# Two-layer decoder trunk on one core: attention scores in visits of four heads, PSUM banks split four and four, sums of squares and their columns at other places

## The chip, the cores and the metric

The kernel runs on one core of a Trainium2 chip. Time is the device time of one execution in microseconds (us). The core's engines appear in the profile as PE (matmul; PEld is its loading of stationary operands), DVE (VectorE), ACT (ScalarE), POOL (GpSimd) and SP (SyncE, which here only issues DMAs). Each engine runs its own queue in order; semaphores make one wait for another.

## The reference, cut to what matters

A sequence of 256 tokens with 1024 channels goes through two layers. Each is: half an FFN step, an attention mixer, half an FFN step, every one on an RMS-normalised copy and added to the stream.

```python
def rmsnorm(x, g):
    return x * lax.rsqrt(jnp.mean(x * x, axis=-1, keepdims=True) + RMS_EPS) * g
def swiglu(h, w_gate, w_up, w_down):
    return (jax.nn.silu(h @ w_gate) * (h @ w_up)) @ w_down
h = h + 0.5 * swiglu(rmsnorm(h, g1), ...)      # D_FF 2816
h = h + mixer(rmsnorm(h, g2))                  # 16 heads of 64
h = h + 0.5 * swiglu(rmsnorm(h, g3), ...)
```

Mixer A (layer 0) is a merged mixture of dilated causal windows; with 256 tokens it comes to one softmax with a mask that holds the logarithm of how many patterns allow a pair. Mixer B (layer 1) is causal attention with keys and values that are projected from the stream after layer 0. A final RMS norm ends it. All is float32.

## The kernel before, in words

**Numbers.** Every float32 operand of a product is split into two parts of a faster format: `hi` is a rounded copy that ACT makes (tiles `wh` for weights, first half of `x`, `pT` and so on), `lo` is the rest, which DVE makes by a subtraction (`wl`). A product is hi*hi + hi*lo + lo*hi, three matmuls into one accumulator (`product`, L189) or, in the FFN, one matmul of 512 columns (hi weights against both halves of x) and one of 256 (lo weights against the hi half; `products_t`, L198: L203 and L206).

**FFN.** `ffn_blocks` (L351) goes over 22 blocks of 128 hidden channels, in pairs that share a load. For each block `both` (L357) makes a gate and an up accumulator: eight hi matmuls of gate, eight hi of up, eight lo of gate, eight lo of up. `close` (L363), traced one block later, adds the two halves of each accumulator (`joined`, L332: a copy by ACT at L335, an add by DVE at L336, after which the bank is free), multiplies by the norm's row, and makes the product silu(gate)*up. The first pair (f = 0) is different: its four accumulators are open at once, and the loop over the eight blocks of x is the outer one. Three of the four come from the pool `accp`, one from `trp`. `quartered` (L449) is the down projection; some of its block pairs go by seven products of quarter blocks, so eight accumulators are open there.

**Norms.** `Norm.scale` makes the two parts of gain*x. `Norm.square` (L234) squares a block on ACT (L237, L240) and POOL adds it to the sum `ss` (L241). `Norm.finish` (L243) makes the column: two float32 matmuls with 1/D (`col`, L246), an addition of epsilon on DVE (L248), a power -0.5 on POOL (L250, `c`). `Norm.spread` turns the column into a row for the FFN (L257, L258, L260). In the very first FFN (`opening`, L172, and `first`, L805) weights and x come in small DMAs; `first` squares blocks two places behind those that it scales, and blocks 6 and 7 are squared behind the loop.

**Mixers.** `mixer` (L722) writes its order out by hand. `projections` (L789) yields 0.68 for every product of three matmuls with 512 columns; six segments of two token halves (t) with eight products each. `Agenda` (L266) holds calls that are due at a time of this count: `evacuate` (L767) scales the finished half by the norm's column (ACT, tile `rt`; DVE rotates it, L635 to L638), `turn_in` (L752) transposes queries and keys (`qt`, L761), `scores(p)` (L649) makes the scores of heads 2p and 2p+1 in two banks, as 12 matmuls that use 64 rows of the array each, one head on each half (L656), and DVE adds the mask and takes the minimum of the negated scores (L664), which frees the banks. `soften`, `scale`, `turn` (L679, transposes `pt`), `values` (L691, accumulator `po`) follow. The lists in the two calls of `mixer` give the waits, counted from the last `turn_in` of a group of four heads. `out_t` (L591) is the output projection, with four accumulators. `Pieces` (L292) loads and splits the projection's weights; `get` keeps four pieces ahead (`LEAD`).

**PSUM.** Eight banks: five in `accp` (accumulators, `acc`), three in `trp` (turns, scores, columns, rows, `trt`). A tile gets a bank of its pool when one is free.

**Order.** The program is traced in the order of the text. The framework then fills each engine's queue ahead of time: among the instructions that it takes to be ready it picks the one that was traced first. `queued(name)` (L145) binds what is traced under it to be queued behind marked instructions of the same engine; nothing waits for them to end. `marks` (L143) holds the marked ones.

The profile drops the numbers in names: `f_g` and `f_u` are the gate and up accumulators of all four FFNs, f10, f20, f11 and f21; `x_n` the scaled x of any norm.

Of the kernel before, what the change touches and what calls it, by code (L numbers as in the profile page):

```python
# [17 lines left out]
NT = S // P  # L18
# [48 lines left out]
def trunk(ctx: ExitStack, tc: tile.TileContext, a: dict, out: bass.AP):  # L67
# [10 lines left out]
    accp = ctx.enter_context(tc.tile_pool(name="accp", bufs=5, space=PS))  # L78
    trp = ctx.enter_context(tc.tile_pool(name="trp", bufs=3, space=PS))
# [92 lines left out]
    def opening(wg, wu, before):  # L172


        for k, n in OPENING:
# [5 lines left out]
            nc.scalar.activation(wh, raw, AF.Copy)  # L181
# [16 lines left out]
    def products_t(acs, wss, xs, first, last):  # L198


        for ac, ws in zip(acs, wss):
            for i, ((wh, wl), x) in enumerate(zip(ws, xs)):
                nc.tensor.matmul(ac, wh, flat(x), start=first and i == 0, stop=False)  # L203
        for ac, ws in zip(acs, wss):
# [14 lines left out]
    class Norm:  # L219
# [23 lines left out]
        def finish(self):  # L243
# [4 lines left out]
            nc.vector.tensor_scalar_add(v, ps[:, :NT], EPS)  # L248
# [43 lines left out]
    class Pieces:  # L292
# [3 lines left out]
        def __init__(self, specs):  # L296
            self.specs, self.raws, self.parts, self.rest = specs, [], [], []
# [9 lines left out]
        def split(self, i):  # L307

            end = 2 * len(self.specs)
            while len(self.parts) <= min(i, end - 1):  # L310
# [10 lines left out]
                while len(self.rest) > (m < end - 1):  # L321
                    self.rest.pop(0)()
# [28 lines left out]
    def ffn_blocks(name, wg, wu, norm, first=None, beside=(), sums=None, queue=()):  # L351
# [5 lines left out]
        def both(f, pair):  # L357
            acs = [acc(f"{name}_{n}{f}") for n in "gu"]
            cols = slice(f % 2 * P, (f % 2 + 1) * P)
            products_t(acs, [[(wh[:, cols], wl[:, cols]) for wh, wl in w] for w in pair], norm.x, True, True)  # L360
# [33 lines left out]
        for f in range(0, KF, 2):  # L394
# [5 lines left out]
            if f == 0:  # L400
# [8 lines left out]
                if first is not None:  # L409
                    for k in range(KD - 2, KD):  # L410
                        norm.square(k)
                if norm.col is None:
                    norm.finish()
# [35 lines left out]
    def quartered(name, w, acts, sums, weight, collected, tail=2):  # L449
# [6 lines left out]
        c11, c12, m1, m5, m7 = [acc(f"dn_{name}_{n}") for n in ("11", "12", "m1", "m5", "m7")]  # L456
        c21, m6, c22 = [trt(f"dn_{name}_{n}") for n in ("21", "m6", "22")]
# [182 lines left out]
    def attention(agenda, operands, mask, name, blocks):  # L640
# [50 lines left out]
        def values(p):  # L691
            g, b = divmod(p, HG // 2)
            po = acc(f"po_{name}{p}")
# [28 lines left out]
    def mixer(name, segs, plan, wo, mask, after, queue={}):  # L722
# [17 lines left out]
        agenda = Agenda()  # L740
        for norm in {id(norm): norm for norm, _, _ in segs}.values():
            for i in range(len(norm.late)):
                agenda.after(1.5 + 0.5 * i, lambda norm=norm: norm.late.pop(0)())
            if norm.col is None:
                agenda.after(8.1, norm.finish)
# [21 lines left out]
        def evacuate(i, t, r, ac, parts):  # L767
# [17 lines left out]
            for g in sorted(set(turned)):  # L785
                if ("q", g, t) in heads and ("k", g, t) in heads:
                    agenda.after(4.4 - 1.2 * t if i == 0 else 3.2, turn_in, g, t)

        def projections():  # L789
            for i, (norm, x, parts) in enumerate(segs):  # L790
                acs = [acc(f"{''.join(part[0] for part in parts)}_{name}{i}_{t}") for t in range(NT)]
                for k0 in range(0, KD, 4):
                    for t in range(NT):
# [4 lines left out]
                        if k0 + 4 == KD:  # L798
                            evacuate(i, t, norm.col[t], acs[t], parts)
# [5 lines left out]
    def first(k, n):  # L805
# [4 lines left out]
        for i in range(k - 2, k - 2 + n):  # L810
            if i >= 0:
                n0.square(i)
# [14 lines left out]
    def ending(at):  # L827
# [3 lines left out]
          [steps(0, 3.0, 8.0, 11.0, 13.8, 16.5, 19.3), steps(1, 3.0, 8.0, 11.0, 13.8, 16.5, 19.3), steps(2, 4.0, 9.2),  # L831
# [92 lines left out]
```

## Time and profile before

| | |
|---|---|
| runs | 980.27, 980.28, 980.37 us (median 980.28) |
| the profiled execution | 980.13 us, of which the span from first to last instruction is 978.4 |
| PE busy | 967.5 us of the span |
| granted PE clock | 0.998 of full speed |

The stages lie on the span like this (from PE's timeline): opening and f10's gate and up products from 5 us; f10's down projection until 190; mixer a until 308; f20 until 489; f11 until 672; mixer b until 789; f21 and the final norm until 978. A timeline row gives start, duration, engine, line, operation, output<-inputs, shapes, and in brackets how long the engine was idle before it and what ended that. Matmuls overlap: their real pace is read from start to start.

### The profile page before, as it was taken

What the parts mean: (1) busy time and instruction counts of PE and PEld (TensorE: products, weight loads), DVE (VectorE), ACT (ScalarE), POOL (GpSimd) and SP (SyncE); (2) the same over time, 40 slices, a digit from 0 to 9 for tenths busy, and PEclk for the clock granted to TensorE, in tenths of its full rate; (3) what the DMA queues carried; (4) which work ended last, traced back from release to release, by engine and by line L of the source; (5) the groups of instructions that cost most, each with busy time, mean ns of one, the idle gap of its engine ahead of it and who ended that gap; (6) DMA issues with size and microseconds to landing.
All of it is one profiled execution on the core that took longest, in us unless ns stands there. A gap on an engine that the chain in (4) does not pass through costs nothing.

```text
span 978.4 us, 14860 instructions
## 1 busy us (share of the span) xinstructions
PE 967.5 (99%) x5391; PEld 831.9 (85%) x5391; DVE 813.0 (83%) x1383; ACT 612.7 (63%) x1131; POOL 287.0 (29%) x242
## 2 busy tenths in 40 slices
PE   8999999999999999999999999999999999999997
PEld 6888888878889888888888888888888998888886
DVE  7988899887878788889898888987787878888995
ACT  7655657567777665556576655655677756666561
POOL 3211246132332211146032121612142322112461
PEclk9999999999999999999999999999999999999999
DMA  9875536664334556546755556483734345564341
GB/s 317 259 238 187 197 133 216 219 212 157 133 98 152 180 186 189 184 153 208 256 172 173 172 177 212 169 277 114 249 131 136 116 145 172 186 202 173 130 172 43
DMA packets 126857, 176.00 MB, mean 180 GB/s; under 512 B 3392, under 2 KB 106304, under 8 KB 126784
## 3 DMA queue, kind: packets, MB, share of 16 engines
q1 hardware_dynamic: 125936, 174.01, 53.7%
q10 hardware_dynamic: 848, 1.05, 0.3%
q8 instruction: 42, 0.69, 0.3%
q14 instruction: 31, 0.25, 0.1%
HBM read 173.99 MB, written 1.05 MB: 179 GB/s over the span
## 4 chain that ended last, share of the span: by engine, by line
PE 92%; DVE 4%; ACT 2%; issue 1%; POOL 1%; DMA 0%; SPq 0%; POOLq 0%; DVEq 0%; ACTq 0%
PE f_g L203 16%; PE f_u L203 16%; PE f_u L206 8%; PE f_g L206 8%; PE dn_f_d L196 6%; PE dn_f_d L192 6%; PE dn_f_d L194 6%; PE dn_f_d_m L196 1%; PE dn_f_d_m L194 1%; PE dn_f_d_m L192 1%; PE qk_a L192 1%; PE qk_a L196 1%; PE qk_a L194 1%; DVE x_n L96 1%; PE q_b L192 1%
## 5 line engine op out<-in xcount | busy, mean ns | idle before, releaser
L368 POOL TENSOR_TENSOR j_f_u<-j_f_u,r_n 128x256 f32<-128x256 f32 x88 | 92.3, 1051 | 360.8 <-DVE j_f_u L336 338.0
L203 PE MATMUL f_g<-x_n,wh_f_g 128*128 128x512 f32 x688 | 180.5, 394 | 0.0
L203 PE MATMUL f_u<-x_n,wh_f_u 128*128 128x512 f32 x688 | 177.2, 390 | 0.0
L203 PEld LDWEIGHTS f_u<-x_n,wh_f_u 128*128 128x128 f32 x688 | 129.2, 188 | 27.3
L203 PEld LDWEIGHTS f_g<-x_n,wh_f_g 128*128 128x128 f32 x688 | 124.0, 189 | 22.7
L167 DVE TENSOR_TENSOR wl_f_u<-raw_f_u,wh_f_u 128x1024 fp32r<-128x1024 f32 x86 | 113.1, 1316 | 1.1 <-ACT wh_f_u L166 1.0
L167 DVE TENSOR_TENSOR wl_f_g<-raw_f_g,wh_f_g 128x1024 fp32r<-128x1024 f32 x86 | 104.3, 1230 | 2.8 <-ACT wh_f_g L166 2.8
L206 PE MATMUL f_u<-x_n,wl_f_u 128*128 128x256 f32 x688 | 103.3, 283 | 0.0
L206 PE MATMUL f_g<-x_n,wl_f_g 128*128 128x256 f32 x688 | 102.7, 282 | 0.0
L206 PEld LDWEIGHTS f_g<-x_n,wl_f_g 128*128 128x128 f32 x688 | 96.4, 190 | 6.3
L166 ACT ACTIVATE wh_f_u<-raw_f_u 128x1024 fp32r<-128x1024 f32 x86 | 88.0, 1049 | 12.0 <-PE f_g L203 7.5
L166 ACT ACTIVATE wh_f_g<-raw_f_g 128x1024 fp32r<-128x1024 f32 x86 | 89.6, 1049 | 4.7 <-PE f_g L203 2.8
L206 PEld LDWEIGHTS f_u<-x_n,wl_f_u 128*128 128x128 f32 x688 | 91.6, 192 | 0.0
L366 ACT ACTIVATE j_f_g<-j_f_g 128x256 f32<-128x256 f32 x88 | 36.7, 417 | 87.2 <-DVE j_f_g L365 86.9
L241 POOL TENSOR_TENSOR ss_n<-ss_n,sq_n 128x256 f32<-128x256 f32 x42 | 38.4, 913 | 148.8 <-ACT sq_n L240 146.8
L98 ACT ACTIVATE act_f<-j_f_g 128x256 fp32r<-128x256 f32 x58 | 23.9, 418 | 56.4 <-DVE j_f_g L376 56.4
L376 DVE TENSOR_TENSOR j_f_g<-j_f_g,j_f_u 128x256 f32<-128x256 f32 x58 | 27.9, 487 | 30.1 <-POOL j_f_u L368 30.1
L484 POOL TENSOR_TENSOR sum_f_d_6b<-sum_f_d_6ac,raw_f_d 128x512 f32<-128x512 f32 x4 | 45.5, 11371 | 17.6 <-DVE sum_f_d_6ac L483 13.2
L336 DVE TENSOR_TENSOR j_f_g<-f_g,j_f_g 128x256 f32<-128x256 f32 x88 | 36.6, 416 | 11.9 <-ACT j_f_g L335 11.9
L677 POOL TENSOR_SCALAR sm_b<-sm_b,ls_b 128x128 f32<-128x128 f32 (+1 forms) x32 | 28.5, 907 | 55.7 <-DVE ls_b L675 29.6
L335 ACT ACTIVATE j_f_u<-f_u 128x256 f32<-128x256 f32 x88 | 33.0, 375 | 15.0 <-PE row_n L258 14.0
L365 DVE TENSOR_TENSOR j_f_g<-j_f_g,r_n 128x256 f32<-128x256 f32 x88 | 41.4, 474 | 0.7
(565 smaller groups left out, 2369.3 us busy)
## 6 DMA issues: line engine op xcount, KB each, us to landing
raw_f_d<-in_ffn_w_down_dram SPq DMA_DIRECT2D x44, 1024.0 KB, 4.9
raw_f_g<-in_ffn_w_gate_dram SPq DMA_DIRECT2D x43, 1024.0 KB, 5.2
raw_f_u<-in_ffn_w_up_dram SPq DMA_DIRECT2D x43, 1024.0 KB, 5.2
raw_qka<-in_a_w_qkv_dram SPq DMA_DIRECT2D x16, 512.0 KB, 4.7
raw_va<-in_a_w_qkv_dram SPq DMA_DIRECT2D x4, 1024.0 KB, 5.4
raw_ao<-in_a_w_o_dram SPq DMA_DIRECT2D x4, 1024.0 KB, 4.9
raw_kvb<-in_kv_w_dram SPq DMA_DIRECT2D x8, 512.0 KB, 4.7
raw_qb<-in_b_w_q_dram SPq DMA_DIRECT2D x4, 1024.0 KB, 5.9
```

Source lines behind the costliest of these rows:

```text
L166: nc.scalar.activation(wh, r, AF.Copy)
L167: nc.vector.tensor_sub(wl, r, wh.bitcast(F32))
L192: nc.tensor.matmul(ac, xh, wh, start=first, stop=False)
L194: nc.tensor.matmul(ac, xh, wl, start=False, stop=False)
L196: nc.tensor.matmul(ac, xl, wh, start=False, stop=last)
L203: nc.tensor.matmul(ac, wh, flat(x), start=first and i == 0, stop=False)
L206: nc.tensor.matmul(ac[:, :S], wl, x[:, 0, :], start=False, stop=last and i == len(ws) - 1)
L241: nc.gpsimd.tensor_tensor(self.ss, self.ss, sq, op=ALU.add)
L365: nc.vector.tensor_mul(g, g, norm.row)
L366: nc.scalar.activation(g, g, AF.Silu)
L368: nc.gpsimd.tensor_tensor(u, u, norm.row, op=ALU.mult)
L484: nc.gpsimd.tensor_tensor(b[:, 0], ac[:, 0], raw[:, 3], op=ALU.add)
```

## The change

- **Banks.** `accp` has four buffers for five, `trp` four for three. `po` of `values` moves from `accp` to `trp`; in the down projection the accumulator m7 does.
- **Scores.** The waits of the two `scores` calls of a group become equal for three of the four groups of each mixer (4.5 and 4.5 for 3.0 and 8.0, and so on), so that both calls run one after the other.
- **Columns in the mixers.** The column of the first segment's norm is due at 8.7 for 8.1, that of another norm at 14.0. After it, the DVE splits of `Pieces` are queued behind the column's addition (`behind`). The evacuation is put on the agenda (at once, or 0.6 later where the column isn't traced yet). `turn_in` of the first segment's second half is due 3.6 behind its evacuation for 3.2.
- **Opening.** `first` only scales. All eight squares are traced behind the opening's loop and queued on ACT behind the last weight split there. The column of this norm is traced in block 2, between gate's hi matmuls and up's (`between`).

```diff
-    accp = ctx.enter_context(tc.tile_pool(name="accp", bufs=5, space=PS))
-    trp = ctx.enter_context(tc.tile_pool(name="trp", bufs=3, space=PS))
+    accp = ctx.enter_context(tc.tile_pool(name="accp", bufs=4, space=PS))
+    trp = ctx.enter_context(tc.tile_pool(name="trp", bufs=4, space=PS))
...
@@ opening
-            nc.scalar.activation(wh, raw, AF.Copy)
+            marks["opening"] = [nc.scalar.activation(wh, raw, AF.Copy)]
...
-    def products_t(acs, wss, xs, first, last):
+    def products_t(acs, wss, xs, first, last, between=None):
         for ac, ws in zip(acs, wss):
             for i, ((wh, wl), x) in enumerate(zip(ws, xs)):
                 nc.tensor.matmul(ac, wh, flat(x), start=first and i == 0, stop=False)
+            if between is not None:
+                between()
+                between = None
...
@@ Norm.finish
-            nc.vector.tensor_scalar_add(v, ps[:, :NT], EPS)
+            marks[self.name] = [nc.vector.tensor_scalar_add(v, ps[:, :NT], EPS)]
...
@@ Pieces
-            self.specs, self.raws, self.parts, self.rest = specs, [], [], []
+            self.specs, self.raws, self.parts, self.rest, self.behind = specs, [], [], [], None
...
-                while len(self.rest) > (m < end - 1):
-                    self.rest.pop(0)()
+                with queued(self.behind):
+                    while len(self.rest) > (m < end - 1):
+                        self.rest.pop(0)()
...
@@ ffn_blocks
-            products_t(acs, [[(wh[:, cols], wl[:, cols]) for wh, wl in w] for w in pair], norm.x, True, True)
+            products_t(acs, [[(wh[:, cols], wl[:, cols]) for wh, wl in w] for w in pair], norm.x, True, True,
+                       norm.finish if norm.col is None else None)
...
                 if first is not None:
-                    for k in range(KD - 2, KD):
-                        norm.square(k)
-                if norm.col is None:
+                    with queued("opening"):
+                        for k in range(KD):
+                            norm.square(k)
+                elif norm.col is None:
                     norm.finish()
...
@@ quartered
-        c11, c12, m1, m5, m7 = [acc(f"dn_{name}_{n}") for n in ("11", "12", "m1", "m5", "m7")]
-        c21, m6, c22 = [trt(f"dn_{name}_{n}") for n in ("21", "m6", "22")]
+        c11, c12, m1, m5 = [acc(f"dn_{name}_{n}") for n in ("11", "12", "m1", "m5")]
+        c21, m6, m7, c22 = [trt(f"dn_{name}_{n}") for n in ("21", "m6", "m7", "22")]
...
@@ values
-            po = acc(f"po_{name}{p}")
+            po = trt(f"po_{name}{p}")
...
@@ mixer
+        def column(norm):
+            norm.finish()
+            pieces.behind = norm.name
...
-                agenda.after(8.1, norm.finish)
+                agenda.after(8.7 if norm is segs[0][0] else 14.0, column, norm)
...
-                    agenda.after(4.4 - 1.2 * t if i == 0 else 3.2, turn_in, g, t)
+                    agenda.after(4.4 - 0.8 * t if i == 0 else 3.2, turn_in, g, t)
...
-                            evacuate(i, t, norm.col[t], acs[t], parts)
+                            agenda.after(0.6 if norm.col is None else 0.0,
+                                         lambda t=t, i=i, norm=norm, ac=acs[t], parts=parts:
+                                         evacuate(i, t, norm.col[t], ac, parts))
...
@@ first
-        for i in range(k - 2, k - 2 + n):
-            if i >= 0:
-                n0.square(i)
...
@@ the calls of mixer: a, then b
-          [steps(0, 3.0, 8.0, 11.0, 13.8, 16.5, 19.3), steps(1, 3.0, 8.0, 11.0, 13.8, 16.5, 19.3), steps(2, 4.0, 9.2),
+          [steps(0, 4.5, 4.5, 11.0, 13.8, 16.5, 19.3), steps(1, 4.5, 4.5, 11.0, 13.8, 16.5, 19.3), steps(2, 5.0, 5.0),
            steps(3, 2.4, 5.4) + ending(8.4)],
...
-          [steps(0, 3.0, 8.0, 11.0, 13.8, 17.0, 19.8), steps(1, 4.0, 9.8, 12.4, 15.2, 17.9, 20.7), [],
-           steps(2, 2.2, 4.3) + steps(3, 6.4, 8.5) + ending(10.4)],
+          [steps(0, 4.5, 4.5, 11.0, 13.8, 17.0, 19.8), steps(1, 5.5, 5.5, 12.4, 15.2, 17.9, 20.7), [],
+           steps(2, 2.4, 2.4) + steps(3, 6.4, 8.5) + ending(10.4)],
```

## The prediction

> **What bounds the kernel now.** I read the page first: engine shares, then the chain that ended last.
>
> ```profile
> PE 967.5 (99%) x5391; PEld 831.9 (85%) x5391; DVE 813.0 (83%) x1383; ACT 612.7 (63%) x1131; POOL 287.0 (29%) x242
> PE 92%; DVE 4%; ACT 2%; issue 1%; POOL 1%; DMA 0%; SPq 0%; POOLq 0%; DVEq 0%; ACTq 0%
> ```
>
> The matmul engine is busy almost everywhere, and the chain runs through it for 92%. The change removes no matmul, so all that can be won is PE's idle time and what it loses between matmuls. The second view is the table by stretches (span, then PE's busy time):
>
> ```profile
> 0.00:14.00 14.00, 11.61 (x44) 6.78 (x45) 8.18 (x15) 10.46 (x21) 4.04 (x10) 1.00 0.90 295
> 26.00:132.00 106.00, 106.00 (x613) 93.70 (x612) 92.09 (x159) 66.62 (x124) 21.10 (x20) 1.00 0.65 213
> ```
>
> In the gate and up products PE has no gap in 106 us; in the opening it lacks 2.4 of 14 us. So only the opening, the two mixers and the seams are open. The third view, PE's waits, gives the largest:
>
> ```profile
> PE f_g L206 <- DVE wl L182: 0.8, 1, 0.8
> PE f_g L203 <- ACT wh L181: 0.8, 2, 0.5
> ```
>
> This view leaves out short gaps, so for the mixers I went down to single rows.
>
> **The norms' columns later.** The timeline of PE has, in mixer a and then in mixer b, the last product ahead of the column and the column (start, duration):
>
> ```profile
> 199.44 0.50 PE L196 MATMUL qk_a<-wh_qka,x_n 128*128 128x512 f32 x1
> 200.04 0.61 PE L246 MATMUL col_n<-mean,ss_n 128*128 128x1 f32 x4
> ...
> 681.45 0.39 PE L196 MATMUL kv_b<-wh_kvb,x_kx 128*128 128x512 f32 x1
> 682.41 0.61 PE L246 MATMUL col_n<-mean,ss_n 128*128 128x1 f32 x4 [0.57 <-POOL ss_n L241]
> ```
>
> In the score rows below, matmuls of 512 columns follow each other every 0.23 us. So PE stood 200.04-199.44-0.23 = 0.37 us in a and 682.41-681.45-0.23 = 0.73 us in b, both for the sum of squares on POOL. The new due times put the column one product (three matmuls, 0.68 us) later in a (8.7 for 8.1) and about nine later in b (14.0): the sums are done before, and other products, which have their weights, fill PE. Gain 1.10 us. In a the column is now late for what follows, the queries' first turn:
>
> ```profile
> 205.15 0.39 PE L196 MATMUL v_a<-wh_va,x_n 128*128 128x512 f32 x1
> 205.76 0.63 PE L761 MATMUL qt_a<-ident,rt_a 128*128 128x128 f32 x4 [0.23 <-ACT wh_qka L318]
> ...
> 207.38 0.40 PE L196 MATMUL v_a<-wh_va,x_n 128*128 128x512 f32 x1
> 207.95 0.63 PE L761 MATMUL qt_a<-ident,rt_a 128*128 128x128 f32 x4 [0.18 <-DVE rt_a L638]
> ```
>
> Two waits, 0.38 and 0.34 us, 0.72 together. They end when the rotated heads are there, that is, by column, variance, power, evacuation, rotation. The edit touches this chain twice: the weight splits on DVE are queued behind the variance (new `behind`), so that it no longer waits for a split, and the first turn is due one product later (the evacuation is deferred by 0.6), the second more (0.8 for 1.2). I count both waits as gone. Behind the variance on DVE stand the splits of pieces that are four ahead of their product (LEAD); a hold of one split hides there. Bounds: 0 and 0.72.
>
> **Scores of four heads in one visit.** One visit of today, on PE:
>
> ```profile
> 211.64 0.39 PE L196 MATMUL v_a<-wh_va,x_n 128*128 128x512 f32 x1
> 211.96 0.33 PE L656 MATMUL s_a<-qkh_a 64*128 64x128 f32 x2
> 212.12 0.28 PE L656 MATMUL s_a<-qkl_a,qkh_a 64*128 64x128 f32 x2
> ...
> 212.63 0.28 PE L656 MATMUL s_a<-qkh_a,qkl_a 64*128 64x256 f32 x2
> 212.85 0.50 PE L192 MATMUL v_a<-wh_va,x_n 128*128 128x512 f32 x1
> 213.18 0.39 PE L194 MATMUL v_a<-wl_va,x_n 128*128 128x512 f32 x1
> ```
>
> Going in costs 211.96-211.64-0.23 = 0.09 us; going out 0.11 (the last pair needs about 0.11 of the 0.22 to 212.85) and 0.10 more, since the first product takes 0.33 to the next instead of 0.23. A visit thus carries 0.30 us beside its twelve matmuls. Two visits in one save one such 0.30 and pay a change from pair to pair, which I take as the 0.05 by which the first change inside a visit (0.16) exceeds 0.11. Three of four groups in two mixers: six times 0.25 = 1.50 us. No row has two visits in a row: bounds 0 (no merging) and 6 x 0.30 = 1.80. The eight reductions that follow load DVE in one block instead of two; nothing waits for them soon, since the first turn stays at 11.0.
>
> A fourth turn bank also removes one wait. The last scores of mixer b:
>
> ```profile
> 759.73 0.73 PE L656 MATMUL s_b<-qkh_b 64*128 64x128 f32 x2
> 760.15 0.43 PE L656 MATMUL s_b<-qkl_b,qkh_b 64*128 64x128 f32 x2
> ...
> 759.66 0.42 DVE L664 CUSTOM_DVE_ANT_0 sm_b<-s_b,masks 128x256 f32<-128x256 f32 x1
> ```
>
> The second head starts only when DVE has read the visit before (760.08): 0.42 instead of 0.16 to the next pair, 0.26 us. Mixers together: 1.10 + 0.72 + 1.50 + 0.26 = **3.58 us less**.
>
> **The bank taken from the accumulators.** Each FFN opens with four accumulators at once, three in `accp` and one in `trp`. With five banks, gate and up of block 2 found two free ones. With four, gate 2 takes the last, and up 2 must wait until DVE has read gate 0 (L336). Here stand when up 2 starts, and that read: f11, with PE's next three items (both low halves, the row, block 3), then f20, f21 and the opening.
>
> ```profile
> 503.91 1.98 PE L203 MATMUL f_u<-x_n,wh_f_u 128*128 128x512 f32 x8
> 505.73 1.12 PE L206 MATMUL f_g<-x_n,wl_f_g 128*128 128x256 f32 x8
> 507.64 0.60 PE L258 MATMUL row_n<-diag_n,ones 128*128 128x128 f32 x4
> 508.00 2.09 PE L203 MATMUL f_g<-x_n,wh_f_g 128*128 128x512 f32 x8
> 507.05 0.42 DVE L336 TENSOR_TENSOR j_f_g<-f_g,j_f_g 128x256 f32<-128x256 f32 x1
> ...
> 321.41 1.99 PE L203 MATMUL f_u<-x_n,wh_f_u 128*128 128x512 f32 x8
> 322.18 0.42 DVE L336 TENSOR_TENSOR j_f_g<-f_g,j_f_g 128x256 f32<-128x256 f32 x1
> ...
> 802.96 1.99 PE L203 MATMUL f_u<-x_n,wh_f_u 128*128 128x512 f32 x8
> 803.73 0.42 DVE L336 TENSOR_TENSOR j_f_g<-f_g,j_f_g 128x256 f32<-128x256 f32 x1
> ...
> 22.23 1.98 PE L203 MATMUL f_u<-x_n,wh_f_u 128*128 128x512 f32 x8
> 24.13 0.42 DVE L336 TENSOR_TENSOR j_f_g<-f_g,j_f_g 128x256 f32<-128x256 f32 x1
> ```
>
> The bank would come 3.56 us late in f11 (507.47 for 503.91), 1.19 in f20 and in f21, 2.32 in the opening. PE has work that needs no bank: gate 2's low half (half of 507.64-505.73, 0.96 us) and the row (508.00-507.64 = 0.36). That the order of a queue follows what is ready, and not the program alone, shows in the opening, where PE's rows run ahead of low halves that DVE hadn't made. So I subtract 1.32: f20 and f21 nothing, f11 **2.24 us more**, as DVE is full with `x_kx` there. Bounds: 0 in all (DVE reads gate 0 first), 3.56 + 1.19 + 1.19 = 5.94 without filler. `po` now shares the turn banks: at most two turns and two outputs, which fit four.
>
> The Trainium skill (Perfetto Trace Analysis, Optimizing Tensor Performance, Matmuls) advises that independent matmul groups rotate through different PSUM banks, so that evacuating one overlaps the next. It speaks against five becoming four at just this place, and the trace agrees: the reads above end after the bank would be wanted.
>
> **The opening's squares later.** Today's rows:
>
> ```profile
> 9.63 0.50 PE L203 MATMUL f_g<-x_n,wh 128*128 128x512 f32 x1 [0.46 <-ACT wh L181]
> 17.28 0.38 PE L206 MATMUL f_g<-x_n,wl 128*128 128x256 f32 x1 [0.81 <-DVE wl L182]
> ...
> 9.61 1.23 DVE L182 TENSOR_TENSOR wl<-raw,wh 128x1024 fp32r<-128x1024 f32 x1 [0.90 <-ACT wh L181]
> 15.47 1.75 DVE L182 TENSOR_TENSOR wl<-raw,wh 128x1024 fp32r<-128x1024 f32 x1
> ...
> 13.18 4.64 POOL L241 TENSOR_TENSOR ss_n<-ss_n,sq_n 128x256 f32<-128x256 f32 x4 [0.47 <-ACT sq_n L240]
> ...
> 18.67 2.01 ACT L166 ACTIVATE wh_f_u<-raw_f_u 128x1024 fp32r<-128x1024 f32 x2 [1.01 <-DMA raw_f_u<-in_ffn_w_up_dram]
> ```
>
> A split on DVE takes 1.23 us alone and 1.75 beside POOL's sums. With the squares behind the last split, ACT and POOL are free of them: the two PE waits, 0.46 + 0.81 = 1.27 us, can go. But block 2 cannot come at will: its up weights land at 18.67, and the read of gate 0 stands behind their splits. If that read stays at 24.13, up 2 starts at 24.55; block 3 follows up 2's two halves (505.73-503.91 = 1.82, and 0.96) later at 27.33; today it starts 1.82 + 1.91 + 0.36 behind 22.23, at 26.32: a loss of 1.0. If it moves up with the rest, the gain is 1.27. The DVE idles ahead of it today for the column, which now comes behind gate 2, so I take a value nearer the gain: **0.7 us less**. At each end: -1.27 and +1.0.
>
> The Trainium skill (SBUF — State Buffer, SBUF: two separate sides) calls the port pair that VectorE (with two SBUF inputs) and GpSimd share an exclusive lock, so the seven sums would hold up block 2's splits as they now hold up the opening's; the trace agrees as to the slowing (1.75 for 1.23).
>
> **The sum.** -3.58 + 2.24 - 0.7 = -2.0 us. The profiled execution took 980.13 us (span 978.4; the median of the runs is 980.28), so **978.1**.
>
> **The rivals.**
> 1. *The wait in order, slower.* If up 2 stays directly behind gate 2 in PE's queue, nothing fills the wait: 5.94 us in f20, f11 and f21, and in the opening the full 2.32. Against 3.58: +4.7, 984.8. It decides from the point where unfilled waits pass 3.6 us. For it: f11's DVE rows; against: PE's order in the opening. Chance 0.15.
> 2. *The banks cost nothing.* The read of gate 0 is scheduled ahead of the splits: -3.58 - 1.27 = -4.9, 975.3. For it: in f20 and f21 the lateness is less than the filler; against: in all four starts of today DVE's read comes after the point where it would be wanted. Chance 0.17.
> 3. *The change doesn't do what it says.* One of four turn banks is still held (a turn, an output) when the visit comes, and it falls apart: 1.5 lost, -0.5, 979.6. For it: mixer b's wait above; against: visits are due 4.5 behind the last turn. Chance 0.18.
> 4. *The slowing moves with the squares.* Seven sums at 4.64/4 = 1.16 us take 8.1 us from the first squares, while up 2, just ahead of which the column stands, starts today 22.23-17.22 = 5.0 us behind the opening's last split: the column waits, and block 2's splits slow down. The opening loses 1.0: -0.3, 979.8. Chance 0.10.
>
> **The numbers.** The forecast has 0.40, mostly between 977 and 979. A measurement of this kernel tells 0.2%, about 2 us, from no change. Faster by more than that (under 978.3): rival 2 and 0.30 of the forecast, 0.47. Within: the rest of the forecast, rivals 3 and 4, 0.38. Slower: rival 1, 0.15. The range leaves out half of rival 1 and some of rival 2's far end (scores at 1.80, a longer gain in the opening): 974.6 to 982.8.
>
> **What would show it.** Column rows right behind a product in both mixers; six fewer changes into the 64-row matmuls, each remaining visit with 24 in a row; up 2 in each FFN start behind gate 2's low half, with a PE wait for DVE's L336 in f11 above 2 us; the opening's waits for `wl` and `wh` gone and sums on POOL between 14 and 22 us. It is wrong if PE waits at the FFN starts reach 4 us together, or if f11 shows none.

## The result and the profile after

The changed kernel takes 993.86 us (median of four runs, 992.73 to 994.84) where the kernel before takes 980.33 beside it: a ratio of 1.0137, 95% interval [1.0122, 1.0152]. It is 13.5 us slower; 978.1 was forecast, and 982.8 was the range's upper end. The profiled execution took 994.84 us with a span of 993.0.

The page of the changed kernel, engine shares and the chain that ended last:

```profile
PE 972.4 (98%) x5391; PEld 837.4 (84%) x5391; DVE 813.7 (82%) x1383; ACT 615.2 (62%) x1131; POOL 291.1 (29%) x242
...
PE 88%; DVE 6%; ACT 3%; issue 1%; DMA 1%; POOL 1%; ACTq 0%; POOLq 0%; SPq 0%; DVEq 0%
```

The same 5391 matmuls are 4.9 us longer busy (967.5 before), so PE not only waits more: it also works more slowly somewhere. On the chain DVE's share has gone from 4 to 6%. The starts of the stages, compared with before, say where: the opening and the gate and up products of f10 lose 5.85 us, mixer a 0.74, f20 0.72, f11's gate and up products 4.14; mixer b wins 1.20 in its products and loses 3.74 in its out-projection; f21 loses 0.72. The down products lose nothing.

PE's waits in the changed kernel (sum, times, longest):

```profile
PE col_n L249 <- POOL ss_n L244: 3.1, 1, 3.1
PE f_u L203 <- DVE j_f_g L340: 3.0, 4, 1.2
PE ot_bo L608 <- DVE ls_b L681: 2.1, 1, 2.1
...
PE row_n L261 <- DVE diag_n L260: 1.1, 2, 0.9
PE qt_a L772 <- DVE rt_a L644: 0.8, 1, 0.8
PE pt_b L688 <- DVE nm_b L670: 0.8, 1, 0.8
```

The four waits of `f_u`, one in each FFN, are the bank that the change took. The column's 3.1 and the out-projection's 2.1 are new. The table by stretches has the rest (span, busy time and instructions of the five engines, then PE's granted clock):

```profile
0.00:14.00 14.00, 12.49 (x48) 8.13 (x49) 7.82 (x16) 9.18 (x16) 0.69 (x6) 1.00 0.88 285
...
26.00:34.00 8.00, 7.15 (x28) 5.82 (x28) 7.51 (x16) 5.46 (x10) 2.11 (x3) 0.67 0.61 184
26.00:132.00 106.00, 105.15 (x593) 92.45 (x593) 89.91 (x157) 66.45 (x120) 21.14 (x20) 0.98 0.64 206
...
516.00:520.00 4.00, 4.00 (x17) 3.56 (x16) 1.94 (x4) 0.25 (x1) 0.00 (x0) 0.58 0.44 132
...
776.00:780.00 4.00, 4.00 (x25) 4.00 (x24) 2.50 (x4) 2.22 (x5) 4.00 (x5) 0.65 0.01 3
```

The same three short stretches in the kernel before:

```profile
26.00:34.00 8.00, 8.00 (x47) 7.00 (x46) 8.00 (x15) 6.71 (x13) 1.63 (x2) 1.00 0.88 281
516.00:520.00 4.00, 4.00 (x27) 3.64 (x26) 3.37 (x8) 2.77 (x5) 0.99 (x2) 1.00 0.02 5
776.00:780.00 4.00, 4.00 (x36) 4.00 (x36) 3.36 (x6) 2.46 (x6) 0.00 (x0) 1.00 0.00 0
```

Behind the waits in the opening, in f11 and in the out-projection the granted clock falls to about 0.6 over the stretch, where it was 1.00, and PE does 17 matmuls in 4 us instead of 27, or 25 instead of 36. Now the single places. First the opening, rows of PE, POOL and DVE:

```profile
18.25 2.07 PE L203 MATMUL f_g<-x_n,wh_f_g 128*128 128x512 f32 x8
23.43 0.61 PE L249 MATMUL col_n<-mean,ss_n 128*128 128x1 f32 x4 [3.11 <-POOL ss_n L244]
23.90 1.62 PE L209 MATMUL f_g<-x_n,wl_f_g 128*128 128x256 f32 x8
25.70 1.22 PE L261 MATMUL row_n<-diag_n,ones 128*128 128x128 f32 x4 [0.18 <-DVE diag_n L260]
27.77 3.71 PE L203 MATMUL f_u<-x_n,wh_f_u 128*128 128x512 f32 x8 [0.85 <-DVE j_f_g L340]
...
14.75 8.63 POOL L244 TENSOR_TENSOR ss_n<-ss_n,sq_n 128x256 f32<-128x256 f32 x7 [13.46 <-ACT sq_n L243]
...
18.16 2.96 DVE L167 TENSOR_TENSOR wl_f_g<-raw_f_g,wh_f_g 128x1024 fp32r<-128x1024 f32 x2 [2.85 <-ACT wh_f_g L166]
```

Block 0's products do end earlier (gate 2 starts at 18.25; in the kernel before the column stood there at 19.93). But the sums on POOL last from 14.75 to 23.38, and the column stands ahead of up 2. Up 2 starts at 27.77 for 22.23 and takes 3.55 us to its low half at 31.32, where 1.82 is normal. Two of block 2's splits take 2.96 beside the sums, 1.48 each; alone one takes 1.23.

Then f11, PE's rows and DVE's:

```profile
513.25 0.46 PE L261 MATMUL row_n<-diag_n,ones 128*128 128x128 f32 x2 [0.90 <-DVE diag_n L260]
514.91 2.87 PE L203 MATMUL f_u<-x_n,wh_f_u 128*128 128x512 f32 x8 [1.20 <-DVE j_f_g L340]
...
513.21 1.22 DVE L167 TENSOR_TENSOR wl_f_u<-raw_f_u,wh_f_u 128x1024 fp32r<-128x1024 f32 x1
514.35 0.42 DVE L340 TENSOR_TENSOR j_f_g<-f_g,j_f_g 128x256 f32<-128x256 f32 x1
```

Up 2 waits for the read of gate 0, which stands on DVE behind the diagonal and a split; the row, which was to fill that wait, now waits itself, because the diagonal is late.

In the mixers the columns and the merged visits came as forecast (mixer a's column, mixer b's column, and the seam between the two halves of one visit):

```profile
206.10 0.39 PE L196 MATMUL qk_a<-wh_qka,x_n 128*128 128x512 f32 x1
206.33 0.50 PE L249 MATMUL col_n<-mean,ss_n 128*128 128x1 f32 x4
...
699.01 0.40 PE L196 MATMUL q_b<-wh_qb,x_n 128*128 128x512 f32 x1
699.25 0.50 PE L249 MATMUL col_n<-mean,ss_n 128*128 128x1 f32 x4
...
220.11 0.28 PE L662 MATMUL s_a<-qkh_a,qkl_a 64*128 64x256 f32 x2
220.23 0.22 PE L662 MATMUL s_a<-qkh_a 64*128 64x128 f32 x2
```

Both columns start 0.23 and 0.24 us behind a product, and the second pair of heads follows the first after 0.12, which is no more than inside a visit. What mixer b loses stands in its out-projection (PE, DVE, ACT):

```profile
773.82 0.35 PE L608 MATMUL ot_bo<-oT_b,wh_bo 128*128 128x256 f32 x1 [2.06 <-DVE ls_b L681]
...
772.80 0.88 DVE L96 SCALAR_TENSOR_TENSOR vs_b<-v_b,c_n,vs_b 128x256 fp32r<-128x256 f32 x2 [0.52 <-ACT vs_b L98]
...
771.88 0.82 ACT L98 ACTIVATE vs_b<-v_b,c_n 128x256 fp32r<-128x256 f32 x2
```

The wait is put down to `ls_b`, a small reciprocal behind it in DVE's queue; what ends at 773.68, just ahead of 773.82, is the evacuation of the last values (`vs_b`). Its accumulator is the bank that the fourth out-accumulator needs; in run 4 below, PE's wait of 1.1 us at this place is put down to `vs_b` itself.

### The profile page after: what moved, and what is told of

It is laid out like the page before. It is cut to its first block, busy times and chain, and to the rows that moved or that the text cites. A ratio compares the mean times of both kernels' runs of the same rounds, so it can differ in the third digit from the quotient of the medians.

```text
span 993.0 us, 14860 instructions
## 1 busy us (share of the span) xinstructions
PE 972.4 (98%) x5391; PEld 837.4 (84%) x5391; DVE 813.7 (82%) x1383; ACT 615.2 (62%) x1131; POOL 291.1 (29%) x242
## 4 chain that ended last, share of the span: by engine, by line
PE 88%; DVE 6%; ACT 3%; issue 1%; DMA 1%; POOL 1%; ACTq 0%; POOLq 0%; SPq 0%; DVEq 0%
PE f_u L203 16%; PE f_g L203 15%; PE f_u L209 8%; PE f_g L209 8%; PE dn_f_d L196 6%; PE dn_f_d L192 6%; PE dn_f_d L194 6%; PE dn_f_d_m L196 1%; PE dn_f_d_m L194 1%; PE dn_f_d_m L192 1%; PE qk_a L192 1%; PE qk_a L196 1%; PE qk_a L194 1%; DVE wl_f_u L167 1%; DVE wl_f_g L167 1%
## 5 line engine op out<-in xcount | busy, mean ns | idle before, releaser
L203 PE MATMUL f_u<-x_n,wh_f_u 128*128 128x512 f32 x688 | 180.1, 394 | 3.0 <-DVE j_f_g L340 3.0
L381 DVE TENSOR_TENSOR j_f_g<-j_f_g,j_f_u 128x256 f32<-128x256 f32 x58 | 25.5, 444 | 31.0 <-POOL j_f_u L373 30.7
L490 POOL TENSOR_TENSOR sum_f_d_6b<-sum_f_d_6ac,raw_f_d 128x512 f32<-128x512 f32 x4 | 42.0, 10502 | 17.6 <-DVE sum_f_d_6ac L489 8.8
L683 POOL TENSOR_SCALAR sm_a<-sm_a,ls_a 128x128 f32<-128x128 f32 (+1 forms) x32 | 29.2, 929 | 50.2 <-DVE ls_a L681 32.6
```

Source lines behind the costliest of these rows:

```text
L490: nc.gpsimd.tensor_tensor(b[:, 0], ac[:, 0], raw[:, 3], op=ALU.add)
L683: nc.gpsimd.tensor_scalar(sm[:, seg], sm[:, seg], ls[:, t:t + 1], None, op0=ALU.mult)
```

## The experiments

My theory A: the loss is a few direct waits (the opening's column for POOL; up 2 for a bank in each FFN; the out-projection for a bank), and behind them the matmul clock at half. Rival B: the mixers' new order is the cost. Rival C: the waits are all, the clock plays no part. Each time below is a median, and "before" is the kernel before, run beside it on the same chip: 980.24 in the first four runs, 980.21 in the next four, 980.44 in the last four.

**1. The opening undone.** The changed kernel with the squares and the column of before:

```diff
         for i in range(k, k + n):
             n0.scale(i)
+        for i in range(k - 2, k - 2 + n):
+            if i >= 0:
+                n0.square(i)
...
                 if first is not None:
-                    with queued("opening"):
-                        for k in range(KD):
-                            norm.square(k)
-                elif norm.col is None:
+                    for k in range(KD - 2, KD):
+                        norm.square(k)
+                if norm.col is None:
                     norm.finish()
```

> The changed kernel with its opening put back (squares early, column ahead of block 2); mixers and banks stay changed. In the trace of the changed kernel the opening to the end of the first gate and up products loses 5.85 us. Theory A (waits, and after them a matmul clock at half): the column's 3.1 us on POOL and the slow stretch behind it go, a bank wait of about 1 us stays at block 2: about 989. Rival B (the mixers' new order is what costs): no more than 1 us back, 992 or more. Rival C (waits alone, the clock plays no part): the opening's waits are 3.11 + 0.18 + 0.85 = 4.1 us against 1.7 won, so about 2.4 us back, 991.4.

Measured: 989.96 us, ratio 1.0099 [1.0084, 1.0114]. So the opening's part is 3.9 us of the 13.5; the time lies between A's 989 and C's 991.4, nearer A. Up to the down products it still loses 1.66, the bank's wait there.

**2. Up 2 in a turn bank.**

```diff
-            acs = [acc(f"{name}_{n}{f}") for n in "gu"]
+            acs = [(trt if f == 2 and n == "u" else acc)(f"{name}_{n}{f}") for n in "gu"]
```

> The changed kernel with the up accumulator of block 2 in a turn bank instead of the fourth accumulator bank, in all four products. Theory A: the four waits for the read of gate 0 go (0.85 in the opening, 1.37 in f11, 0.6 to 0.7 in f20 and f21), and in f11 the row's wait of 1.05 is covered by up 2 as before and the half clock behind both goes too: f11 gets back its 4.1 us, all together about 6: 987 to 988. Rival C: the waits alone, 0.85 + 1.05 + 1.37 + 1.3 = 4.6, so 989.3. Rival B: the mixers are the cost, under 2 us back, 992.

Measured: 988.12, ratio 1.0071 [1.0054, 1.0088]. In its trace f11 loses nothing (0.04 for 4.14), f20 and f21 nothing; the opening still 5.65, since its column waits as before. That is near A's 987 to 988, but the four runs lie between 985.59 and 989.03, and C's 989.3 is not far.

**3. The two waits filled.** Matmuls that compute nothing, in the opening between gate 2 and the column and in f11 between gate 2's low half and up 2:

```diff
+    def stuff(n, last):
+        scrap = trt("stuff")
+        with tc.issue_after(last.ins):
+            for i in range(n):
+                nc.tensor.matmul(scrap, fill[:, :P], fill, start=True, stop=True)
```

> The changed kernel with matmuls that compute nothing (a constant by itself into a spare bank) in two of its waits: 13 between gate 2 and the column in the opening, 10 between gate 2's low half and up 2 in f11. At 0.227 us each they take 2.95 and 2.27 us, no longer than the waits they stand in. Theory A: the waits stay as long, but the clock does not fall to half behind them: about 3 us back in the opening and 1.5 to 2 in f11, 988 to 990. Rival C: nothing changes or it gets a little slower, 993 to 995. The stretch at half clock in the second mixer's out-projection has no filler and stays in both.

Measured: 994.66, ratio 1.0148 [1.0133, 1.0164]: by the time alone, C. The stretches tell the two places apart (span, PE busy, granted clock):

```profile
29.00:34.00 5.00, 4.81 (x14) 0.50 0.89 281
508.00:516.00 8.00, 7.95 (x47) 1.00 0.70 222
516.00:520.00 4.00, 3.62 (x20) 1.00 0.35 105
```

In f11 the clock stays at 1.00 where it was 0.58, and the stage loses 2.84 for 4.14. In the opening there is now another wait, and half clock behind that:

```profile
27.28 0.77 PE L270 MATMUL row_n<-diag_n,ones 128*128 128x128 f32 x4 [1.61 <-DVE diag_n L269]
29.19 3.78 PE L207 MATMUL f_u<-x_n,wh_f_u 128*128 128x512 f32 x8 [1.13 <-DVE j_f_g L349]
```

The filler changed DVE's order: a split slipped between the variance and the diagonal, and the power on POOL took 1.62 us instead of 0.71 beside it. So f11 agrees with A, though in one trace only; the opening tells nothing, and the time misses A's 988 to 990.

**4. The banks alone.** The kernel before with four banks of each kind:

```diff
-    accp = ctx.enter_context(tc.tile_pool(name="accp", bufs=5, space=PS))
-    trp = ctx.enter_context(tc.tile_pool(name="trp", bufs=3, space=PS))
+    accp = ctx.enter_context(tc.tile_pool(name="accp", bufs=4, space=PS))
+    trp = ctx.enter_context(tc.tile_pool(name="trp", bufs=4, space=PS))
...
-            po = acc(f"po_{name}{p}")
+            po = trt(f"po_{name}{p}")
```

(and `m7` of the down products to a turn bank).

> The kernel before with four accumulator and four turn banks (one accumulator of the down products and the mixers' outputs moved to turn banks) and nothing else. Theory A: block 2's up waits for the read of gate 0 in all four products: f11 +4.1 with the half clock, f20 and f21 +0.7 each, the opening +1 to +2.3; 986.5 to 988.5. Rival B: banks cost little, the mixers' order does: 980 to 982. Rival C: the waits alone: f11 +2.4, f20 and f21 +1.4, opening +1: 985.

Measured: 986.76, ratio 1.0068 [1.0053, 1.0083], 6.5 us slower with nothing else changed. B is out as the main cause. The time lies in A's range, but not by A's account: in this trace the clock stays at 1.00, and f11 loses 2.62 (C expected 2.4, A 4.1), the opening 1.72, f20 and f21 0.7 each, and the out-projection 0.94, which neither had counted. The trace makes a pair with that of run 1, f11 in both; here the rows of the banks alone:

```profile
508.20 0.46 PE L258 MATMUL row_n<-diag_n,ones 128*128 128x128 f32 x2 [0.89 <-DVE diag_n L257]
509.87 2.09 PE L203 MATMUL f_u<-x_n,wh_f_u 128*128 128x512 f32 x8 [1.21 <-DVE j_f_g L336]
```

and of run 1, the opening undone:

```profile
509.18 0.46 PE L261 MATMUL row_n<-diag_n,ones 128*128 128x128 f32 x2 [0.93 <-DVE diag_n L260]
510.84 3.61 PE L203 MATMUL f_u<-x_n,wh_f_u 128*128 128x512 f32 x8 [1.21 <-DVE j_f_g L340]
```

The same two waits, once with up 2 at 2.09 us and once at 3.61. The fall of the clock does not follow from the length of the waits alone. What differs is where they lie. In every trace here the granted clock changes only at whole steps of 3.413 us from its first change to 1.00 (in run 1 this fall comes 148 steps behind it). Two such steps of run 4 (span, PE busy, granted clock), and then of run 1:

```profile
504.58:507.99 3.41, 2.73 (x16) 1.00 1.06 365
507.99:511.40 3.41, 1.99 (x9) 1.00 0.61 194
```

```profile
507.59:511.00 3.41, 1.27 (x9) 1.00 1.03 332
511.01:514.41 3.40, 3.40 (x9) 0.50 0.12 30
```

In run 4 the two waits are spread over two steps, with 0.68 and 1.42 us of idleness; in run 1 both lie in one step, with 2.14, and the next step runs at half clock. The fourteen traces have eleven falls, not counting the one at the end of each. Each stands behind a step in which PE was idle for 1.6 to 2.4 us; 1.42 brought none, and one step with 1.84 (run 8) brought none either. This is read from the traces as they are: no run moved a wait against the steps on purpose.

**5. The mixers alone.** Runs 1 and 2 together: the opening of before, up 2 in a turn bank. What is left of the change is the mixers.

> The changed kernel with the opening put back and block 2's up accumulator in a turn bank: what is left of the change is the mixers. From the stages of the runs so far: the four products as before, mixer a 0.7 to 0.9 us longer, mixer b 1.2 shorter in its products and 3.7 longer in its out-projection. Theory A: 983 to 984. Rival C (no clock): the out-projection's wait of 2.06 alone, 981.8. Rival B': the mixers did gain their 3.58 us and other stages took it: 976.7.

Measured: 982.70, ratio 1.0028 [1.0017, 1.0039], seven runs from 981.85 to 984.09. That is just under A's 983 to 984 and above C's 981.8. The seven are of two kinds: four (981.85 to 982.70) with a mean granted clock of 0.998 or 0.999, and three (983.52 to 984.09) with 0.997; the trace is of the longest of these. The mixers as changed cost 2.5 us instead of saving 3.6.

**6. Direct evacuation.** As run 5, but deferred only where the column isn't there yet:

```diff
-                            agenda.after(0.6 if norm.col is None else 0.0,
-                                         lambda t=t, i=i, norm=norm, ac=acs[t], parts=parts:
-                                         evacuate(i, t, norm.col[t], ac, parts))
+                            if norm.col is None:
+                                agenda.after(0.6, lambda t=t, i=i, norm=norm, ac=acs[t], parts=parts:
+                                             evacuate(i, t, norm.col[t], ac, parts))
+                            else:
+                                evacuate(i, t, norm.col[t], acs[t], parts)
```

> As the kernel of the run with the mixers alone, but an accumulator is evacuated at once wherever the norm's column exists, as in the kernel before; only the first segment's evacuation still waits for its column. Theory A: the last segment's evacuation in mixer b is no longer queued behind the last scores, the out-projection's wait for the bank falls from 2.06 to the 1.1 us of the run with the banks alone, without the half clock: b's out-projection +1 instead of +3.7, so 2.7 us less than with the mixers alone, about 981. Rival: the wait comes from having four banks and the order of evacuation does not matter: no difference between the two.

Measured: 980.04, ratio 0.9997 [0.9988, 1.0006], 2.7 us less than run 5, as A expected: the order of evacuation was the cost. A had put all of it into the out-projection. By the stages of the two traces, the out-projection loses 1.41 for 3.74 (where the clock had fallen), but mixer a also wins 1.12 where it lost 0.72, and mixer b's products win only 0.6 for 1.2. A deferral by 0.0 is a place in the agenda behind what is due already, here behind the last scores. A wait that the kernel before does not have is left in mixer a, rows of ACT, DVE and PE:

```profile
245.85 1.05 ACT L321 ACTIVATE wh_va<-raw_va 128x1024 fp32r<-128x1024 f32 x1
...
246.94 1.48 DVE L323 TENSOR_TENSOR wl_va<-raw_va,wh_va 128x1024 fp32r<-128x1024 f32 x1 [0.79 <-ACT wh_va L321]
...
249.93 0.63 PE L771 MATMUL qt_a<-ident,rt_a 128*128 128x128 f32 x4 [0.81 <-DVE rt_a L643]
```

The rotation of the heads stands behind this split on DVE, the split waits for ACT, and ACT has first to get through the eight exponentials of the merged visit, which end at 245.85; in run 7, with four of them, the same split on ACT starts at 243.27. In mixer b a turn waits 0.53 because the merged scores hold all four turn banks until DVE has read the first: the read ends at 723.99, the turn starts at 724.05.

**7. The columns alone.** The kernel before with the new due times, the splits behind the variance and the turn at 0.8, five accumulator banks, evacuation as in run 6:

```diff
-                agenda.after(8.1, norm.finish)
+                agenda.after(8.7 if norm is segs[0][0] else 14.0, column, norm)
...
-                    agenda.after(4.4 - 1.2 * t if i == 0 else 3.2, turn_in, g, t)
+                    agenda.after(4.4 - 0.8 * t if i == 0 else 3.2, turn_in, g, t)
```

> The kernel before (five accumulator banks, its opening, its single scores) with the later columns alone: due 8.7 and 14.0, the splits queued behind the variance, the second turn at 0.8, and the first segment's evacuation deferred only where its column is not there yet. The prediction's terms for it are 1.10 for the columns and 0.72 for the queries' turns. Theory A: they come, 978.5. Rival: the later column delays what follows as much as it wins: 980.0 to 980.5.

Measured: 978.23, ratio 0.998 [0.997, 0.999]: 2.0 us faster, against 1.82 forecast for these terms. This part alone beats both kernels.

**8. The column behind up 2.** Run 2, with the opening's column behind up 2's high half:

```diff
-            if between is not None:
+            if between is not None and ac is acs[-1]:
                 between()
-                between = None
```

> The changed kernel with block 2's up accumulator in a turn bank (as one earlier run), and the opening's column behind up 2's high half instead of ahead of it. The eight matmuls of up 2, 1.82 us, then stand in the column's wait of 3.1 us. Theory A: the wait falls to about 1.3 us, and with it the half clock behind it (in the earlier run the opening lost 5.65 us, 2.25 of them counted at half clock): the opening loses 1 to 2 us, so 4 us less than the 988.1 of that run: 984. Rival C (no clock): 1.8 us less: 986.3.

Measured: 984.27, ratio 1.0038 [1.0023, 1.0053]; run 2 had 988.12. The waits left in the opening:

```profile
22.91 0.61 PE L248 MATMUL col_n<-mean,ss_n 128*128 128x1 f32 x4 [0.78 <-POOL ss_n L243]
...
27.17 2.11 PE L203 MATMUL f_g<-x_n,wh_f_g 128*128 128x512 f32 x8 [1.22 <-DVE j_f_g L339]
```

Eight matmuls, 1.82 us together, put into the column's wait bring 3.9 us. Most of the rest is the clock: it was at half for 6.83 us in the opening of run 2's trace and stays at 1.00 in this one (gate 3 at 2.11, normal), which is of the quickest of the four executions, 982.69. The time is A's 984, not C's 986.3. The same trace has the out-projection's wait, here with the clock kept:

```profile
763.93 0.35 PE L607 MATMUL ot_bo<-oT_b,wh_bo 128*128 128x256 f32 x1 [2.06 <-DVE ls_b L680]
...
765.50:768.90 3.40, 3.40 (x31) 1.00 0.13 40
```

The stage loses 2.16 where run 5 loses 3.74 with the same wait of 2.06. By the steps of run 4, PE is idle for 1.84 us of one step here and for 2.06 in run 5.

**9. The merges undone.** Run 6 with the scores in single visits again (the due times of before in the plans).

> As the run with direct evacuation (980.04), but the scores in single visits again: what is left is the later columns and the four banks. Theory A (the merges win about 2 us on the matmul engine, and the new waits behind them, 0.97 for the rotated heads, 0.70 and 0.26 for the turn banks, take most of it back): within 0.5 us of 980.0, so the merges are worth nothing net. Rival: the merges keep the 1.5 us forecast: 981.5. Rival: they only cost: 978.8 or less.

Measured: 979.33, ratio 0.9989 [0.9979, 0.9998], 0.7 less than with the merges, a little outside the 0.5 that A allowed. In the traces the merges save 1.12 us of PE's time in mixer a and 0.89 in b, about 2.0 against 1.5 forecast; so the waits that come with them must cost about 2.7.

**10. The out-projection's wait filled.** Run 5 with nine matmuls that compute nothing ahead of the fourth out-accumulator:

```diff
+                if (name, i, j, k) == ("bo", 3, 0, 0):
+                    scrap = trt("stuff")
+                    with queued("step"):
+                        for _ in range(9):
+                            nc.tensor.matmul(scrap, fill[:, :P], fill, start=True, stop=True)
```

> The kernel of the run with the mixers alone (982.7), with nine matmuls that compute nothing (0.227 us each, 2.04 in all) in the one wait of 2.06 us in mixer b's out-projection. Nothing else waits there, so this is the clock alone. Theory A: the wait is filled, the matmuls behind it run at 0.12 instead of 0.21 us, the 1.17 us counted at half clock come back and the runs spread less: 981.4 to 981.7. Rival C: the filler changes nothing or costs some tenths: 982.7 to 983.

Measured: 982.24, ratio 1.0018 [1.0008, 1.0027], ten runs from 982.02 to 982.65. The stretches of run 5 (PE busy, granted clock), and then of this one:

```profile
761.00:764.00 3.00, 0.94 (x14) 1.00 0.46 134
764.00:768.00 4.00, 4.00 (x23) 0.57 0.47 163
```

```profile
761.00:764.00 3.00, 2.93 (x19) 1.00 0.65 200
764.00:768.00 4.00, 4.00 (x36) 1.00 0.33 114
```

36 matmuls instead of 23 in the same 4 us: the clock stays at 1.00, and the out-projection loses 2.17 for 3.74. This one trace doesn't show that the filler did it, since run 8's kept the clock without any and lost 2.16. The ten executions say more: their mean granted clock is 0.998 to 1.000 in all, where three of run 5's seven had 0.997. The median falls by only 0.5, not by 1.0 to 1.3 as expected, because the clock fell in only those three of run 5's executions; against the other four the filler wins nothing, as the wait stays as long.

**11. The opening mended.** Run 7 with the opening of the change, the column behind up 2's high half, and the read of gate 0 and up 0 traced right behind block 0:

```diff
+                if first is not None:
+                    acs[0] = [joined(ac, f"{name}_{n}0") for ac, n in zip(acs[0], "gu")] + [True]
                 done += [(i, *acs[i]) for i in range(2)]
```

> The kernel with the columns alone (978.23) and the opening of the change, mended in two places: the column stands behind up 2's high half, and the read of gate 0 and up 0 stands ahead of the column's chain, as soon as block 0's products end. Theory A: the opening's gain in its own products (18.2 for 19.9 at the end of block 0) is no longer lost to the wait for the sums and to the wait for gate 0's bank; block 3 starts 0.3 to 0.7 earlier than before: 977.5 to 978.0. Rival: the slowed splits of block 2 (1.7 instead of 1.2 us beside the sums) hold up its low halves: 978.3 to 979.5.

Measured: 978.41, ratio 0.9978 [0.9969, 0.9987], the same as run 7. A's 977.5 to 978.0 is missed, the rival's 978.3 to 979.5 holds. Up 2 now waits 0.3 for its split weights and the column 0.8 for POOL; block 3 starts at 26.57, in run 7 at 26.61. The opening's edit wins nothing, even so.

**12. The opening alone** on the kernel before, with five accumulator banks (the opposite of run 1's diff).

> The kernel before with the opening of the change alone, five accumulator banks. Up 2 has its bank; the column stands ahead of it and waits for the sums. Theory A: the same loss as in the run with up 2 in a turn bank, +5.65: 985.9, and the runs apart by more than those of the kernel before. Rival C: the waits alone, about 3.1 + 0.2 against 1.7 won and what the row's chain shifts: 982 to 983.6. Prediction's rival 4 had +1.0: 981.2.

Measured: 985.3, ratio 1.0049 [1.0035, 1.0063], runs from 984.04 to 986.51. The column waits 2.7 us, and the stage loses 4.06 in the profiled execution, the quickest of the four. That is near A's 985.9 and above C's 982 to 983.6. In this trace the clock is at half for one step of 3.41 us, behind a wait of 2.70; in run 2's, behind one of 2.74, for two steps, and the stage loses 5.65.

## Why the prediction was wrong

One ladder of the runs, each against the kernel before beside it, puts a price on each part in this order: columns -1.98 (run 7); the four banks in the mixers +0.87 (run 9); the merges +0.94 (run 6); the deferred evacuation +2.66 (run 5); the bank at the FFN starts +7.23 (run 1); the opening on top +3.81 (the change). Sum +13.53.

- **Columns and first turns, -1.82: right.** Measured -1.98; by the distance of matmuls -1.16 in mixer a and about -0.8 in b, for 1.09 and 0.73.
- **Merged scores, -1.50 and -0.26: the saving right, the cover wrong.** PE saved about 2.0 us. The step that failed is "The eight reductions that follow load DVE in one block instead of two; nothing waits for them soon, since the first turn stays at 11.0": the eight exponentials behind them held up the next splits on ACT and with them the rotation on DVE, and the scores held turn banks for which the next turn waited.
- **The evacuation: a step that wasn't priced.** I counted "the evacuation is deferred by 0.6" as part of the first turn and did not follow what 0.0 does to all others. In mixer b it queued the last one behind the last scores.
- **The bank, +2.24 (bounds 0 to 5.94): +7.23 and +0.87.** The place was right: up 2 stands behind gate 2's low half. f11's wait for the read is 1.20, though, and only with the row's 0.90 above the 2 us that were named as a sign. In f11 the size was near: run 4's trace, at full clock, loses 2.62 there, and the half clock makes it 4.14 in the changed kernel. The step "PE has work that needs no bank: gate 2's low half [...] and the row" failed for the row: it depends on DVE as the read does; in f11 it waited 0.90 itself, in f20 it came behind up 2. "f20 and f21 nothing" became 0.7 each, and the opening's start, which had no bank term, lost 1.72 in run 4. The out-projection's four accumulators were not priced at all (+0.87 in the mixers by run 9; run 4's out-projection lost 0.94).
- **The opening, -0.7 (ends -1.27 and +1.0): +4.9** alone (run 12), +3.8 on four banks, +5.4 with up 2 in a turn bank (run 2 against run 5). The step "I take a value nearer the gain" failed. The mechanism was that of rival 4; its price of 1.0 left out that PE, whose queue has the column ahead of up 2, has nothing else to do while the sums run to 23.4. It also left out the clock. The Trainium skill (SBUF — State Buffer, SBUF: two separate sides) has the exclusive lock that the prediction cites. The trace agrees as to the slowing again, 1.48 for 1.23 in the splits, but that was the smaller part.
- **The clock: in no term and no rival.** The granted clock was 1.00 in every stretch I had quoted, so I priced a wait by its length. Behind three waits in the changed kernel matmuls of 512 columns follow each other at 427 ns from start to start instead of 227, and in the out-projection those of 256 columns at 213 instead of 119, for one step of 3.41 us in f11 and in the out-projection and for two in the opening. A step at half clock costs 1.5 to 1.6 us: 4.14 against 2.62 in f11 (the changed kernel and run 4), 3.74 against 2.16 in the out-projection (runs 5 and 8), 5.65 against 4.06 in the opening (runs 2 and 12). By that, the four steps of the changed kernel's profiled execution are about 6 of the 14.6 us by which its span is longer, an estimate. The Trainium skill (TensorE: Matmul & The Clock Gate, What's actually happening) says that the clock is at half by default and after about 3.4 us of idleness, in windows that run freely, and is released after as long a busy time. The traces agree on the factor, on the length of a window (their steps of 3.41 us) and on its running freely (run 4 and run 1, where the same waits lie in two steps and in one). They differ on the idleness: a single wait of 2.06 us was enough in run 5, and in run 1 two of 0.93 and 1.21 us. By the Trainium skill's figure neither would reach a window; the measurement decides.

The prediction's own test spoke correctly: it was to be wrong "if PE waits at the FFN starts reach 4 us together"; they are 4.1 with the row's, beside the column's 3.1. Rival 1, the only slower one, expected up 2 directly behind gate 2, which did not happen; its time, 984.8, is nearer than the forecast, but for another reason.

Two smaller points of the prediction: in the view of PE's waits before, the largest is 1.4 us for `fill`, ahead of the first matmuls; it was left out, and is the same in every run. The forecast that the sums on POOL end by 22 us took 1.16 us for each; they took 1.23 and ended at 23.4.

What stays open: how much idleness in one step makes the clock fall. Single waits of 0.7 to 1.2 us (runs 6, 8, 9) did not bring it in the profiled executions; the out-projection's 2.06 did in five traces and not in run 8's.

## What to carry to other kernels

A bank, like an engine, is priced at every place where all of them are taken: list those places (four FFN starts and an out-projection here), and ask of each filler whether it depends on the same late engine. On a matmul engine that is never idle, a wait of two microseconds can cost more than its length, since 3.41 or 6.83 us at half clock may follow it, at 1.5 to 1.6 us for each 3.41; a granted clock under 1.00 in the table by stretches and a spread of runs that grows to 2 us are its signs. And when an edit has several parts, the part that frees an engine (here the later column, 2.0 us by itself) is worth trying without the parts that take something away.

## What was not expected of the hardware

- A granted clock of 0.50 for 3.41 or 6.83 us right behind waits of 1.6 to 3.1 us, one or two together; eight matmuls of 1.82 us took up to 3.57 (run 3).
- The clock changes on a grid of 3.41 us that does not follow the program: two waits in one step brought the fall (run 1), the same two in neighbouring steps did not (run 4).
- With matmuls on constants in the wait, the clock stayed at 1.00 behind it in the traces of runs 3 (f11) and 10, and no execution of run 10 had a mean under 0.998.
- One program loses the clock in some of its executions: run 4 has three at 986.63 to 986.82 with a mean of 0.999 and one at 987.66 with 0.996. No two traces of one program show it.
- A change from one pair of heads to the next costs nothing beyond the pace (0.12 us from start to start), where 0.05 had been estimated.
- A power of 128x2 values on POOL took 1.62 us beside a split on DVE and 0.71 without one (run 3 against the changed kernel).
